# Convolution tables loaded earlier, the first two row tiles of an output projection written in two parts, and cache copies moved beside the residual's loads

## The chip, the cores and the metric

The kernel runs on one NeuronCore of a Trainium2 chip. The metric is device time in microseconds (us). The engines are PE (TensorE, the matrix products), DVE (VectorE), ACT (ScalarE), POOL (GpSimd) and SP (SyncE, which here only issues DMAs). DMAs issued by SP go through queue q1 and those issued by POOL through queue q0, the "software" queue; in the profile both show up on the same 16 DMA engines.

## What is computed

One layer of a hybrid decoder: RMSNorm, an input projection, gated linear attention and dilated attention, an output projection with residual, RMSNorm, a ConvFFN with residual, and a final RMSNorm. 544 tokens go through it: 512 of a prompt and 8 x 4 of samples. What the change touches, cut from the reference:

```python
D_MODEL = 2048; D_FF = 5504; CONV_W = 3
# o:  the attention's heads side by side, 16 blocks of 128 columns
h  = x + o @ w_out                                  # output projection and residual
u  = rmsnorm(h) @ w_up                              # 2 x 5504 columns
c  = causal depthwise conv of u, width 3, its first rows from state_ffn_conv
y  = h + (silu(gate(c)) * up(c)) @ w_dn             # down projection and residual
# k_sample, v_sample: the caches shifted by 4 rows, with the new rows put behind
```

## The kernel before, in words

All matrices are kept transposed: 128 rows of the model's width on the partitions, the 544 tokens along a row. A product in nearly full precision is made of three products of halves: each weight tile `raw` is split by ACT into `whi` (line 190) and by DVE into `wlo` (line 191), each operand likewise into a high and a low tile, and PE multiplies high by high, high by low and low by high. `wpart` loads 8 blocks of 128x128 of a weight (512 KB, issued by SP at line 846) and splits them; `gemm` (line 225) multiplies a list of such units.

A scheduler (the tile framework, with a timeline simulation) sets the order of instructions on each engine, so the order written in the program is a proposal. A DMA queue serves what is put on it in the order of issue. Tiles are allocated from pools with a fixed number of buffers, and a write waits until the buffer's last reader is done.

Four stages matter here.

- **Output projection** (about 840 to 1060 us). A loop over 16 row tiles `ot`, line 930: `gemm` of two units with the operands `og` (16 of them, of which the last two are ready last). DVE adds the PSUM tile to the residual `h`, loaded by POOL from `xT` (lines 935, 936); POOL writes the sum to `hscr` in DRAM (line 937); at every odd `ot`, `keep_rows()` puts one copy of 3060 KB, DRAM to DRAM, on POOL's queue (line 634), a piece of `k_sample` or `v_sample`. 16 such copies are made in the whole kernel, 10 of them in earlier stages and 6 here.
- **ConvFFN, up projection** (about 1060 to 1986 us). 43 pairs of column tiles. Each product (`product`, line 965) goes through the steps p1 to p7 of a `Pair`, in a fast-multiplication scheme that makes operands by additions. After the first tiles' statistics `rstd` are ready, POOL loads the convolution's table `vcv` (line 1086) and the first states `ci` (line 1101); ACT copies the states into the tiles `F` (line 1028).
- **Down projection.** First a short `gemm` over three kept pairs (16 row tiles), then three groups of pairs, each with 16 row tiles of 12 us. The activations come back from DRAM (`ar <- adr`, SP, line 1141) into `NSLOT` slots of one pool and 24 - `NSLOT` of another. In the first group the residual is added: SP loads `hr <- hscr[ot]` (line 1202), DVE adds it.
- **End.** The final norm and the outputs.

Of the kernel before, what the change touches and what calls it, by code (L numbers as in the profile page):

```python
# [17 lines left out]
P = 128  # L18
# [24 lines left out]
GATES_FIRST = 4  # L43
POOL_SPLIT = 6
NKEPT = 3
NSLOT = 11
FW = 2 + TP + NB * (2 + TS)


# [74 lines left out]
def _build(tc, nc, es, xT, st_gla, ck, cv, conv_in, vecs, w_in, w_gu, w_out, w_up, w_dn,  # L124
# [172 lines left out]
    def gps():  # L297
        return pg.tile([P, 2, 512], F32, tag="g", name="g")
# [551 lines left out]
    def wpart(w, ks, c0):  # L850
        with tc.high_priority(offset=min(PO, tc.cur_priority - P0)):
            n = len(ks)
            raw = wraw()
            wload(raw, w, ks, c0)
            hi, lo = wsplit(raw, n)
        return [(k, hi[:, i, :], lo[:, i, :]) for i, k in enumerate(ks)]
# [38 lines left out]
    def factors(some, X, pool):  # L895
# [24 lines left out]
        for i in some:  # L920
# [3 lines left out]
            else:  # L924
                parts(i, T3, 2, b[i][:, 1:3])

    X = {}
    for ot in range(KD):
        ps = gps()
        gemm(ps, [wpart(w_out, order[:8], ot * P), wpart(w_out, order[8:], ot * P)], og)  # L930
        i, j = divmod(ot, 2)
        if j == 0:
            hp = HX.tile([P, 2, NT], F32, tag="h", name="h", bufs=KD // 2 + 1 - AHEAD)
        ht = hp[:, j]
        nc.gpsimd.dma_start(ht, xT[ot * P:(ot + 1) * P, :])
        nc.vector.tensor_add(hv(ht), hv(ht), ps[:, :, :HT])
        nc.gpsimd.dma_start(hscr[ot], ht)
        if ot == 0:
            nc.scalar.activation(acc2, ht, AF.Square)
        else:  # L940
            sq = htmp("sq")
            nc.scalar.activation(sq, ht, AF.Square)
            nc.vector.tensor_add(acc2, acc2, sq)
        X[i] = hp
        if ot % 2 == 1 and kept_rows:
            keep_rows()
        nc.scalar.activation(ht, ht, AF.Copy, scale=vec[:, V_FFN + ot:V_FFN + ot + 1])
        if j == 1 and i < AHEAD:
            factors([i], X, VA)
# [27 lines left out]
    class Pair:  # L977
# [79 lines left out]
        def conv(self):  # L1057
            out = []
            for s, F in ((0, self.Fu), (1, self.Fg)):
# [22 lines left out]
    nc.scalar.activation(rstdF[:, 2:2 + TP], rstd[:, :TP], AF.Copy)  # L1082
    nc.scalar.activation(rstdF[:, 2 + TP:].rearrange("p (b s) -> p b s", s=2 + TS)[:, :, 2:],
                         rstd[:, TP:].rearrange("p (b t) -> p b t", t=TS), AF.Copy)
    vcv = FP.tile([P, NVEC - V_CW], F32, name="vcv")
    nc.gpsimd.dma_start(vcv, vecs[:, V_CW:])

    ci_v = conv_in.rearrange("p (s f) r -> p s f r", s=2)
    co_v = conv_out.rearrange("p (s f) r -> p s f r", s=2)
    def sv(x):  # L1090
        return x[:, 2 + TP:].rearrange("p (b s) -> p b s", s=2 + TS)[:, :, :TS]

    KEPT = list(range(KF - 1 - NKEPT, KF - 1))
    kept = {}
    ci = co = None
    for f, pr in enumerate(pairs):
        if f % 4 == 0:
            n = min(4, KF - f)
            ci = FP.tile([P, 2, 4, 2 * NB], F32, tag="ci", name="ci", bufs=2)
            co = FP.tile([P, 2, 4, 2 + 2 * NB], F32, tag="co", name="co", bufs=2)  # L1100
            nc.gpsimd.dma_start(ci[:, :, :n, :], ci_v[:, :, f:f + n, :])
        pr.ci, pr.co = ci[:, :, f % 4, :], co[:, :, f % 4, :]
        if f:
            pr.p5()
# [85 lines left out]
    for gi, ks in enumerate(groups):  # L1190
        A = {}
        with tc.high_priority(offset=min(2000, tc.cur_priority - P0)):
            for k in ks:
                A[k] = A1[k] if k in A1 else fetch(k, where[k])
        if gi < len(groups) - 1:
            for ot in range(KD):
                ps = gps()
                gemm(ps, [wpart(w_dn, ks[i:i + 8], ot * P) for i in range(0, len(ks), 8)], A)
                nc.vector.tensor_add(hv(h[ot]), hv(h[ot]), ps[:, :, :HT])
                if gi == 0:  # L1200
                    x = W3.tile([P, NT], F32, tag="hr", name="hr", bufs=1)
                    nc.sync.dma_start(x, hscr[ot])
                    nc.vector.tensor_add(h[ot], h[ot], x)


# [116 lines left out]
```

## Time and profile before

| | |
|---|---|
| median of 3 runs | 2526.18 us (2524.59 to 2527.97) |
| the profiled execution's own time | 2525.1 us |
| its span | 2523.3 us, so 1.8 us lie around it |
| mean granted TensorE clock | 0.991 of full speed |
| PE busy | 2462.7 us, 98% of the span |

The span is what the views of the trace cover; sums are made against the profiled execution's 2525.1 us, which is 1.1 us under the median. The granted clock is given in shares of 2.4 GHz; at its lower level, 1.2 GHz, it reads 0.5.

### The profile page before, as it was taken

The page shows a single profiled execution, that of the slowest core. Times are in us where ns is not written, and L with a number is a line of the kernel's source. Part 1 is how long each engine was busy: PE and PEld are TensorE (multiplying, and loading weights), DVE is VectorE, ACT ScalarE, POOL GpSimd, SP SyncE. Part 2 cuts the span into 40 slices and gives each one's busy share as a digit, 9 for nine tenths or more (in the row PEclk, how much of TensorE's full clock was granted, in tenths as well). Part 3 has the DMA queues.
Part 4 walks back from the last instruction along what each step waited for, and adds up shares of the span by engine and source line. Part 5 has one row for each costly group of instructions (what it writes and reads, how often), then busy time and mean ns, then how long its engine had stood idle before and what let it go on. Part 6 is the DMA issues. An engine that isn't in the chain of part 4 may idle for free.

```text
span 2523.3 us, 47163 instructions
## 1 busy us (share of the span) xinstructions
PE 2462.7 (98%) x19479; PEld 2385.2 (95%) x19479; DVE 1619.3 (64%) x2460; ACT 1078.8 (43%) x1870; POOL 435.3 (17%) x581
## 2 busy tenths in 40 slices
PE   8999999999999899989999999999999999999997
PEld 8988887899999899989999999999999999999997
DVE  7777764267777843478878888888888643342243
ACT  6344464133334433355555555555555531131142
POOL 1333434210002320112212221222121000000001
PEclk9999999999999999999999999999999999999999
DMA  7777744544555498668888888889888473443232
GB/s 220 197 202 197 193 114 138 161 131 141 166 177 177 159 305 256 169 146 192 192 188 192 191 191 189 191 191 192 189 191 178 124 219 107 115 151 92 85 100 72
DMA packets 581593, 427.73 MB, mean 170 GB/s; under 512 B 18976, under 2 KB 553728, under 8 KB 580608
## 3 DMA queue, kind: packets, MB, share of 16 engines
q1 hardware_dynamic: 462144, 248.31, 34.9%
q0 software_dynamic: 115200, 171.02, 30.1%
q10 hardware_dynamic: 4032, 5.38, 0.6%
q8 instruction: 153, 2.51, 0.4%
q14 instruction: 64, 0.52, 0.1%
HBM read 397.40 MB, written 77.37 MB: 188 GB/s over the span
## 4 chain that ended last, share of the span: by engine, by line
PE 82%; DMA 8%; DVE 6%; issue 2%; POOL 1%; ACT 1%; SPq 0%; DVEq 0%; POOLq 0%; ACTq 0%
PE g L225 40%; PE b L965 20%; PE g L965 15%; DMA q<-qscr 6%; DVE pr L411 1%; PE v L507 1%; PE s L673 1%; DMA ar<-adr 1%; DVE wlo L191 1%; DVE kv L412 1%; PE s L561 1%; DMA xr<-in_xT_dram 0%; PE s L548 0%; PE s L795 0%; POOL q L408 0%
## 5 line engine op out<-in xcount | busy, mean ns | idle before, releaser
L191 DVE TENSOR_TENSOR wlo<-raw,whi 128x1024 fp32r<-128x1024 f32 (+1 forms) x341 | 408.3, 1198 | 295.6 <-ACT whi L190 288.7
L190 ACT ACTIVATE whi<-raw 128x1024 fp32r<-128x1024 f32 (+1 forms) x345 | 355.0, 1030 | 555.1 <-PE g L225 454.0
L225 PE MATMUL g<-ah,whi 128*128 128x272 f32 x2048 | 442.9, 296 | 9.8 <-ACT ah L190 4.6
L225 PE MATMUL g<-al,whi 128*128 128x272 f32 x2048 | 447.2, 297 | 0.5 <-DVE al L191 0.5
L225 PE MATMUL g<-ah,wlo 128*128 128x272 f32 x2048 | 442.4, 295 | 0.3 <-DVE wlo L191 0.3
L965 PE MATMUL b<-vh,whi 128*128 128x272 f32 x1376 | 395.1, 288 | 6.2 <-ACT V L1038 4.8
L965 PE MATMUL b<-vl,whi 128*128 128x272 f32 x1376 | 395.9, 289 | 0.8 <-DVE vl L893 0.6
L965 PE MATMUL b<-vh,wlo 128*128 128x272 f32 x1376 | 389.9, 288 | 1.3 <-DVE wlo L191 1.3
L225 PEld LDWEIGHTS g<-ah,whi 128*128 128x128 f32 x2048 | 327.9, 191 | 19.7 <-issue 10.3
L225 PEld LDWEIGHTS g<-al,whi 128*128 128x128 f32 x2048 | 329.2, 191 | 11.6 <-issue 9.3
L225 PEld LDWEIGHTS g<-ah,wlo 128*128 128x128 f32 x2048 | 328.3, 190 | 10.2 <-issue 8.5
L965 PE MATMUL g<-vl,whi 128*128 128x272 f32 x1032 | 298.8, 290 | 2.0 <-DVE vl L893 1.9
L965 PE MATMUL g<-vh,whi 128*128 128x272 f32 x1032 | 297.8, 289 | 0.4 <-ACT vh L892 0.3
L965 PE MATMUL g<-vh,wlo 128*128 128x272 f32 x1032 | 296.8, 288 | 0.0
L965 PEld LDWEIGHTS b<-vh,whi 128*128 128x128 f32 x1376 | 260.0, 189 | 6.7 <-ACT V L1038 5.1
L225 PE MATMUL g<-dh,whi 128*128 128x272 f32 x1248 | 258.0, 288 | 4.1 <-ACT whi L190 2.7
L965 PEld LDWEIGHTS b<-vl,whi 128*128 128x128 f32 x1376 | 259.5, 189 | 1.5 <-DVE vl L893 1.5
L965 PEld LDWEIGHTS b<-vh,wlo 128*128 128x128 f32 x1376 | 257.4, 189 | 1.5 <-DVE wlo L191 1.5
L225 PE MATMUL g<-dh,wlo 128*128 128x272 f32 x1248 | 258.2, 288 | 0.0
L225 PE MATMUL g<-dl,whi 128*128 128x272 f32 x1248 | 258.1, 288 | 0.0
L190 ACT ACTIVATE whi<-rs 128x1024 fp32r<-128x1024 f32 x129 | 136.8, 1061 | 266.8 <-PE g L965 201.1
L225 PEld LDWEIGHTS g<-dh,whi 128*128 128x128 f32 x1248 | 195.7, 188 | 5.4 <-ACT whi L190 3.4
(341 smaller groups left out, 4101.5 us busy)
## 6 DMA issues: line engine op xcount, KB each, us to landing
raw<-in_w_up_dram SPq DMA_DIRECT2D x129, 512.0 KB, 4.1
raw<-in_w_in_dram SPq DMA_DIRECT2D x96, 512.0 KB, 4.8
raw<-in_w_dn_dram SPq DMA_DIRECT2D x64, 512.0 KB, 4.0
out_k_s_dram<-in_ck_dram POOLq DMA_DIRECT2D x8, 3060.0 KB, 12.7
out_v_s_dram<-in_cv_dram POOLq DMA_DIRECT2D x8, 3060.0 KB, 14.5
ra<-in_w_up_dram SPq DMA_DIRECT2D x43, 512.0 KB, 7.9
rs<-in_w_up_dram SPq DMA_DIRECT2D x43, 512.0 KB, 3.8
rs<-in_w_up_dram POOLq DMA_DIRECT2D x43, 512.0 KB, 9.8
```

Of the source, the lines that this page charges most:

```text
L190: nc.scalar.activation(hi, src, AF.Copy)
L191: eng.tensor_sub(lo, src, hi.bitcast(F32))
L225: nc.tensor.matmul(ps[:, s, :HT], a, b[:, s * HT:(s + 1) * HT], start=(i == 0 and n == 0), stop=(i == len(todo) - 1 and n == 2))
L411: nc.vector.tensor_mul(pr, kt[:, 4:5, :].broadcast_to([P, TS, QC]), q5[:, 1:5, :])
L412: nc.vector.tensor_mul(kt[:, 0:4, :], kt[:, 0:4, :], q5[:, 0:1, :].broadcast_to([P, 4, QC]))
L507: nc.tensor.matmul(psv[32 * m:32 * m + 32, :QC], lhs, rhs, start=(kt == 0), stop=(kt == 5), tile_position=(0, 32 * m))
L561: nc.tensor.matmul(psc[r, :P], vt[:, j * P + 64 * e:j * P + 64 * e + 64], t[:, j * P:(j + 1) * P], start=(j == 0), stop=(j == qi))
L673: nc.tensor.matmul(ps[:, c * P:(c + 1) * P], KS[:, c * P:(c + 1) * P], Q[:, :, c * 64:(c + 1) * 64], start=True, stop=True)
L965: nc.tensor.matmul(b[:, :HT], a_[:, i, :], x_[i][:, v, :], start=(first and i == 0 and n == 0), stop=(i == 7 and n == 2), skip_group_check ...
```

## The change

Five edits. (1) `vcv` and the first `ci` are allocated from another pool and loaded by POOL before the output projection's first `h` load; (2) the first two row tiles of the output projection are written as two passes: units up to the last two operands for both tiles, then the last two for both; (3) the six last copies leave the output projection and are issued at odd `ot` of the first group of the down projection; (4) the loads `hr` go from SP's queue to POOL's and get two buffers in place of one; (5) `NSLOT` is 10 in place of 11.

```diff
-NSLOT = 11
+NSLOT = 10
...
+    vcv = wu.tile([P, NVEC - V_CW], F32, name="vcv")
+    nc.gpsimd.dma_start(vcv, vecs[:, V_CW:])
...
+    def states(f):
+
+        n = min(4, KF - f)
+        ci = wu.tile([P, 2, 4, 2 * NB], F32, tag="ci", name="ci", bufs=2)
+        co = wu.tile([P, 2, 4, 2 + 2 * NB], F32, tag="co", name="co", bufs=2)
+        nc.gpsimd.dma_start(ci[:, :, :n, :], ci_v[:, :, f:f + n, :])
+        return ci, co
+
+    state = states(0)
+
+    def two_tiles(w, order, X, n):
+
+        out = []
+        for ot in range(2):
+            units = [u for ks in (order[:8], order[8:]) for u in wpart(w, ks, ot * P)]
+            out.append((gps(), units))
+        for part in range(2):
+            for ps, units in out:
+                m = len(units) - n
+                for i, (k, hi, lo) in list(enumerate(units))[m * part:(m, None)[part]]:
+                    xh, xl = X[k]
...
     X = {}
+    starts = two_tiles(w_out, order, og, 2)
     for ot in range(KD):
-        ps = gps()
-        gemm(ps, [wpart(w_out, order[:8], ot * P), wpart(w_out, order[8:], ot * P)], og)
+        if ot < 2:
+            ps = starts[ot]
+        else:
+            ps = gps()
+            gemm(ps, [wpart(w_out, order[:8], ot * P), wpart(w_out, order[8:], ot * P)], og)
...
-        if ot % 2 == 1 and kept_rows:
-            keep_rows()
...
-    vcv = FP.tile([P, NVEC - V_CW], F32, name="vcv")
-    nc.gpsimd.dma_start(vcv, vecs[:, V_CW:])
...
                 if gi == 0:
-                    x = W3.tile([P, NT], F32, tag="hr", name="hr", bufs=1)
-                    nc.sync.dma_start(x, hscr[ot])
+                    x = ctile("hr")
+                    if ot % 2 == 1 and kept_rows:
+                        keep_rows()
+                    nc.gpsimd.dma_start(x, hscr[ot])
                     nc.vector.tensor_add(h[ot], h[ot], x)
```

What this makes of the instructions' order is shown at three places. Line numbers of the changed kernel are about 30 higher than those of before.

The first place is the first two row tiles of the output projection. On PE, the changed kernel's rows for their last two operands (`ah_9199` and `ah_9203`, with their low halves `al_`) read:

```order
L955 MATMUL g<-ah_9199,whi 128x272 x4
L955 MATMUL g<-al_9200,whi 128x272 x2
L955 MATMUL g<-ah_9199,wlo 128x272 x2
L955 MATMUL g<-ah_9203,whi 128x272 x2
L955 MATMUL g<-al_9200,whi 128x272 x2
L955 MATMUL g<-ah_9199,wlo 128x272 x2
```

Before, these rows stand at the same numbers in the same order, with L225 for L955; so do the rows ahead of them back to the start of both tiles: the scheduler had already put the two tiles into each other. On DVE, at the evacuation of these tiles, before:

```order
L191 TENSOR_TENSOR al_9204<-oa,ah_9203 128x544
L191 TENSOR_TENSOR wlo<-raw,whi 128x1024
L936 TENSOR_TENSOR h<-h,g 128x544
L191 TENSOR_TENSOR wlo<-raw,whi 128x1024
L936 TENSOR_TENSOR h<-h,g 128x544
L943 TENSOR_TENSOR acc_9278<-acc_9278,sq 128x544
```

And changed:

```order
L191 TENSOR_TENSOR al_9204<-oa,ah_9203 128x544
L191 TENSOR_TENSOR wlo<-raw,whi 128x1024 x2
L972 TENSOR_TENSOR h<-h,g 128x544 x2
L979 TENSOR_TENSOR acc_9278<-acc_9278,sq 128x544
L191 TENSOR_TENSOR wlo<-raw,whi 128x1024
```

A second weight split now stands ahead of the first evacuation.

The second place is ACT at the first pair's end, where the states enter `F` and the next weights are split. Before:

```order
L1017 ACTIVATE U_11440<-b0_11320 128x272
L1082 ACTIVATE rstdF_11402<-rstd_77 128x512
L1083 ACTIVATE rstdF_11402<-rstd_77 128x8x4
L1028 ACTIVATE F_11472<-ci_11408 128x8x2
L1028 ACTIVATE F_11473<-ci_11408 128x8x2
L190 ACTIVATE whi_11582<-raw_11580 128x1024
L1038 ACTIVATE V_11511<-b0_11320 128x272
```

And changed:

```order
L1051 ACTIVATE U_11434<-b0_11319 128x272
L1062 ACTIVATE F_11466<-ci_9281 128x8x2
L1062 ACTIVATE F_11467<-ci_9281 128x8x2
L1116 ACTIVATE rstdF_11401<-rstd_77 128x512
L1117 ACTIVATE rstdF_11401<-rstd_77 128x8x4
L190 ACTIVATE whi_11576<-raw_11574 128x1024
L1072 ACTIVATE V_11505<-b0_11319 128x272
```

The copies from `ci` moved ahead of the two `rstdF` copies, and their load is now issued some 200 us earlier in the program.

The third place is the start of the down projection's first group. SP before, around its first residual load:

```order
L846 DMA raw_22656<-in_w_dn_dram 128x8x128
L846 DMA raw_22769<-in_w_dn_dram 128x8x128
L1141 DMA ar<-adr_9247 128x544
L1202 DMA hr<-hscr_9219 128x544
L1141 DMA ar<-adr_9248 128x544
```

In the changed kernel SP has the same rows without the `hr` row, and POOL, whose list before had nothing behind its last `adr` store but the final products, goes on like this:

```order
L1147 DMA adr_9277<-a 128x544
L1230 DMA hr<-hscr_9219 128x544
L634 DMA out_k_s_dram<-in_ck_dram 48x16320
L1230 DMA hr<-hscr_9220 128x544
L1230 DMA hr<-hscr_9221 128x544
L634 DMA out_v_s_dram<-in_cv_dram 48x16320
L1230 DMA hr<-hscr_9222 128x544
L1230 DMA hr<-hscr_9223 128x544
L634 DMA out_k_s_dram<-in_ck_dram 48x16320
```

The first `hr` load waits for PE's last product of the kept pairs; the first copy and the second `hr` load wait for nothing else; the third waits for DVE's addition of the first. So the first copy goes out right behind the first `hr` load, when the kept pairs end, and that is also when SP issues `raw_22656`.

## Rows read from the trace of the kernel before

**Rows 1.** Windows: length; busy of PE, PEld, DVE, ACT, POOL; clock, DMA share, GB/s.

```profile
900.00:1050.00 150.00, 150.00 (x1197) 150.00 (x1196) 63.02 (x86) 52.07 (x71) 14.20 (x24) 1.00 0.83 255
...
1090.00:1100.00 10.00, 5.03 (x24) 4.49 (x23) 4.28 (x6) 3.21 (x8) 2.02 (x2) 0.70 0.82 163
1100.00:1950.00 850.00, 850.00 (x6795) 850.00 (x6794) 678.97 (x929) 439.82 (x769) 169.12 (x218) 1.00 0.88 189
...
2020.00:2030.00 10.00, 9.14 (x72) 8.73 (x70) 3.40 (x4) 3.57 (x7) 0.00 (x0) 1.00 1.04 295
2030.00:2040.00 10.00, 8.69 (x55) 8.47 (x56) 4.77 (x5) 4.16 (x5) 0.00 (x0) 0.83 0.87 257
```

**Rows 2.** Timeline of PE, 1087 to 1101: start, duration, [idle before <- releaser].

```profile
1090.47 0.29 PE L965 MATMUL b<-vh,wlo 128*128 128x272 f32 x1
1095.60 0.60 PE L965 MATMUL b<-vh,whi 128*128 128x272 f32 x1 [4.85 <-ACT V L1038]
...
1097.16 0.43 PE L965 MATMUL b<-vh,wlo 128*128 128x272 f32 x1
1097.39 0.43 PE L965 MATMUL b<-vh,whi 128*128 128x272 f32 x1
```

**Rows 3.** Timeline of ACT, 1084 to 1097.

```profile
1088.48 0.64 ACT L1082 ACTIVATE rstdF<-rstd 128x512 f32<-128x512 f32 x1 [3.73 <-DVE rstdF L1081]
...
1094.00 0.32 ACT L1028 ACTIVATE F<-ci 128x16 f32<-128x16 f32 x2 [4.77 <-DMA ci<-in_conv_in_dram]
1094.23 1.04 ACT L190 ACTIVATE whi<-raw 128x1024 fp32r<-128x1024 f32 x1
1095.17 0.38 ACT L1038 ACTIVATE V<-b 128x272 f32<-128x272 f32 x1
```

**Rows 4.** Timeline of POOL, 1076 to 1099; an issuing row's duration is that of the issue.

```profile
1088.35 0.59 POOL L1086 DMA_DIRECT2D vcv<-in_vecs_dram  x1 [2.01 <-DVE rstd L171]
1088.92 0.73 POOL L1101 DMA_DIRECT2D ci<-in_conv_in_dram  x1
```

**Rows 5.** Timeline of POOL, 874 to 900.

```profile
883.48 4.31 POOL L935 DMA_DIRECT2D h<-in_xT_dram  x8 [17.29 <-issue]
```

**Rows 6.** Timeline of PE, 880 to 897.

```profile
881.56 1.27 PE L225 MATMUL g<-ah,whi 128*128 128x272 f32 x4 [4.55 <-ACT ah L190]
889.82 0.79 PE L225 MATMUL g<-ah,whi 128*128 128x272 f32 x2 [3.14 <-DVE h L936]
```

**Rows 7.** Timeline of DVE, 874 to 900.

```profile
888.95 0.72 DVE L936 TENSOR_TENSOR h<-h,g 128x544 f32<-128x544 f32 x1 [0.66 <-DMA h<-in_xT_dram]
889.59 1.22 DVE L191 TENSOR_TENSOR wlo<-raw,whi 128x1024 fp32r<-128x1024 f32 x1
```

**Rows 8.** Timeline of SP, 2012 to 2050.

```profile
2023.21 1.46 SPq L846 DMA_DIRECT2D raw<-in_w_dn_dram  x2
```

**Rows 9.** DMA issue at 2023.2: KB, us to landing.

```profile
raw<-in_w_dn_dram SPq DMA_DIRECT2D x1, 512.0 KB, 6.7
```

**Rows 10.** Timeline of ACT, 2028 to 2033.

```profile
2030.02 2.00 ACT L190 ACTIVATE whi<-raw 128x1024 fp32r<-128x1024 f32 x2 [1.09 <-DMA raw<-in_w_dn_dram]
```

**Rows 11.** Timeline of PE, 2028 to 2032.

```profile
2031.13 0.52 PE L225 MATMUL g<-dh,whi 128*128 128x272 f32 x2 [1.99 <-ACT whi L190]
```

**Rows 12.** DMA, 919.5 to 931, a copy in flight: packets, MB, share of engines.

```profile
q0 software_dynamic: 136, 3.36, 87.7%
q1 hardware_dynamic: 487, 0.25, 9.1%
```

**Rows 13.** DMA, 894 to 906, loads and a copy on q0 mixed.

```profile
q0 software_dynamic: 1402, 3.35, 95.6%
q1 hardware_dynamic: 1935, 0.97, 34.8%
```

**Rows 14.** DMA issues around 919.0: a load half a microsecond behind a copy, KB, us to landing.

```profile
out_v_s_dram<-in_cv_dram POOLq DMA_DIRECT2D x1, 3060.0 KB, 12.5
raw<-in_w_out_dram SPq DMA_DIRECT2D x1, 512.0 KB, 14.4
```

More of the change, by code (lines that the diff above doesn't have):

```diff
@@ L925, in factors @@
                 parts(i, T3, 2, b[i][:, 1:3])
+    vcv = wu.tile([P, NVEC - V_CW], F32, name="vcv")
+    nc.gpsimd.dma_start(vcv, vecs[:, V_CW:])
+    ci_v = conv_in.rearrange("p (s f) r -> p s f r", s=2)
+    co_v = conv_out.rearrange("p (s f) r -> p s f r", s=2)
+    def states(f):
[15 more added lines that the diff above has]
+                    xh, xl = X[k]
+                    for j, (a, b) in enumerate(((hi, xh), (hi, xl), (lo, xh))):
+                        for s in range(2):
+                            nc.tensor.matmul(ps[:, s, :HT], a, b[:, s * HT:(s + 1) * HT], start=(i == 0 and j == 0),
+                                             stop=(i == len(units) - 1 and j == 2), skip_group_check=True)
+        return [ps for ps, units in out]
     X = {}
+    starts = two_tiles(w_out, order, og, 2)
     for ot in range(KD):
-        ps = gps()
-        gemm(ps, [wpart(w_out, order[:8], ot * P), wpart(w_out, order[8:], ot * P)], og)
+        if ot < 2:
[3 more added lines that the diff above has]
+            gemm(ps, [wpart(w_out, order[:8], ot * P), wpart(w_out, order[8:], ot * P)], og)
         i, j = divmod(ot, 2)
@@ L1084, in _build @@
                          rstd[:, TP:].rearrange("p (b t) -> p b t", t=TS), AF.Copy)
-    vcv = FP.tile([P, NVEC - V_CW], F32, name="vcv")
-    nc.gpsimd.dma_start(vcv, vecs[:, V_CW:])
-    ci_v = conv_in.rearrange("p (s f) r -> p s f r", s=2)
-    co_v = conv_out.rearrange("p (s f) r -> p s f r", s=2)
     def sv(x):
@@ L1094, in _build @@
     kept = {}
-    ci = co = None
     for f, pr in enumerate(pairs):
         if f % 4 == 0:
[L1098 to L1101, printed above, removed]
+            ci, co = states(f) if f else state
         pr.ci, pr.co = ci[:, :, f % 4, :], co[:, :, f % 4, :]
```

## The prediction, made before the changed kernel ran

> **What bounds the kernel now.** The page says that PE is busy for 98% of the span; about 60 us are idle, so what this change can give lies in a few waits of PE and in the clock behind them. I therefore read the busy windows by stage first, to see where PE waits at all, then the timelines around each wait, and last the DMA queues. The windows [rows 1] show two long stretches with nothing to win: the output projection from 900 to 1050 and the up projection from 1100 to 1950 have PE busy to the last hundredth at full clock. 150 us hold 1197 matmuls there, so a matmul costs 0.125 us at full clock. In 1090 to 1100 PE is busy for 5.03 us only, at a clock of 0.70; in 2020 to 2040 it idles too, and the DMA engines are saturated (share 1.04, 295 GB/s) as nowhere else in these rows. These two places, with the start of the output projection, are the ones where the edits land.
>
> **Edit 1, the early table and states: a gain of 6.2 us.** PE stops after the matmul at 1090.47 and goes on at 1095.60, having waited 4.85 us for ACT's `V` [rows 2]. On ACT [rows 3] `V` stands behind the split `whi`, and that behind the copies `F<-ci`, which waited 4.77 us for the states' DMA. POOL issued it at 1088.92, just after the table, because `vcv` had waited for `rstd` [rows 4]. In the changed kernel the states are loaded 200 us earlier, so `F<-ci` waits for nothing but `rstd`, which is there before 1088.48. What is late next: the split `whi` of 1.04 us needs a buffer that PE's running product reads until shortly before its end, and `V` (0.38 us) needs that end itself, 1090.47 + 0.29 = 1090.8. If `whi` runs from 1090.1 to 1091.2, `V` ends at 1091.55 and PE goes on at about 1091.6. Its wait shrinks from 4.85 to 0.8: 4.05 us. Then the clock: the matmuls behind the long wait come every 0.23 us (1097.16, 1097.39 [rows 2]), which is the level of 1.2 GHz. The 24 matmuls of that window would take 3.0 us at 0.125 instead of 5.03, which is 2.0 lost; with an estimated 0.2 for the first ones behind 1100 it is 2.2 us, which I count as gained, since a wait of 0.8 us is short. Sum 6.2. Ends: 3.5, if half of the wait's remainder stays with another operand and the clock falls all the same (4.85 - 1.35); 7.05, if nothing is left at all. The up projection behind it is PE-bound [rows 1], so the gain is kept.
>
> The same edit puts the table and two loads of states ahead of the first `h` load on POOL's queue. POOL stood idle ahead of those loads for 17 us and began them at 883.48 [rows 5]. The three new issues take 0.59 + 0.73 + 0.73 = 2.05 us; how much of that fits into the idle time depends on when their buffers come free, so the `h` load is late by 0 to 2.05 us. What this costs is taken with the next edit, where the load is waited for.
>
> **Edit 2, two tiles in two passes: 0, with a loss of 0.7 beside it.** PE waits 4.55 us up to 881.56 for the last operands and 3.14 us up to 889.82 for the first evacuation [rows 6]. The passes would fill the first wait if PE took up other work there. But the instructions on PE stand in the same order as before, the two tiles being already interleaved: both waits have what they had ahead of them. On DVE, the second `wlo` (1.22 us) now stands ahead of the first evacuation, which had ended at 889.67 after waiting 0.66 us for its residual's load [rows 7], the one that POOL issues from 883.48 on. If that `wlo` starts where DVE had been waiting, at about 888.29, it ends at 889.5 and the evacuation starts 0.55 us later than before; the later load adds a little if it is late by more than 0.5. I take +0.7; ends 0 and +2.05.
>
> **Edit 3 at its old place: 0.** The copies delayed loads there, but PE waited for nothing from 900 to 1050 [rows 1]; a quicker load gives nothing.
>
> **Edits 3 and 4 at their new place: a loss of 9 us.** The kept pairs' products end at about 2023.2. SP then issues two weight loads, at 2023.21 [rows 8]; the first takes 6.7 us [rows 9], ACT starts to split it at 2030.02 after 1.09 us of waiting [rows 10], and PE stands still for 1.99 us until 2031.13 for that split [rows 11]. So here a DMA ends last, and every microsecond that this load comes later is one more for PE, which has done by then what it could do without it. The first `hr` load on POOL is released by the same event, takes 0.55 us to issue, and the first copy follows, at about 2023.8 to 2024.3. It brings 3.13 MB to engines that are full.
>
> How much the copy holds up the load is the disputed price. With a copy alone on q0 [rows 12], 11.5 us moved 3.36 MB for q0 and 0.25 MB for q1: 292 and 22 GB/s. The copy's 3.13 MB take 10.7 us, in which q1 gets 0.24 MB in place of the 3.15 MB of 295 GB/s, so that it is thrown back by 9.9 us. With small-row loads mixed into q0 [rows 13] q1 got 0.97 MB in 12 us, 81 GB/s, which throws it back by 10.7 - 2.9 = 7.8 us. The `hr` load's 272 KB, earlier than before, add up to 0.9. A load of 512 KB issued half a microsecond behind a copy landed after 14.4 us [rows 14], 7.7 later than the 6.7 of ours. These say 7.7 to 10.8; I take 9, because our load has something like 2 us of head start before the copy's data move. Ends: 0, if it lands before; 13.4, if the copy's whole 12.5 us of issue to landing and the 0.9 lie ahead.
>
> The Trainium skill's page "DMA: Bandwidth & Descriptors" says in its section "Queues, rings and completion order" that each DMA engine takes turns between the queue rows at the granularity of packets, so that big packets take more of it. Our rows agree in kind: per packet in the trace q0 moved 25 KB and q1 0.5 KB, although the turns were not equal in number (136 to 487). Read as equal shares of the bytes the rule would make this loss about 4.5, not 9.
>
> The clock behind this wait is already 0.83 in 2030 to 2040 [rows 1], so a longer wait adds little there. Later copies come every 24 us behind an addition of DVE, the rhythm which the output projection bore at 150 of 150 us [rows 1], and the third and later `hr` loads have 24 us for themselves: 0. What covers them is the weights' buffers, filled ahead; if that cover is gone, each of the five costs what the first does.
>
> **Edit 5: 0.** The number of loads is the same and their order on SP keeps its rows; PE's order takes 60 matmuls of the second row tile ahead of the last operands of the first, so a late activation has 7.5 us of cover.
>
> **Sum.** -6.2 + 0.7 + 0 + 9 + 0 = +3.5 us. On the profiled execution's 2525.1 that is 2528.6; its median stands 1.1 us higher, so the forecast for the median is 2529.7, rounded to 2529.5. About 5 us (0.2%) is what a measurement of this kernel can tell from no change, so the likeliest outcome is "the same, a little slower".
>
> **Rivals**, all as medians (2526.2 plus the sum).
>
> - *Even shares.* The load and the copy share the engines evenly. The load has about 4.6 us left when the copy's data start, and needs twice that: +4.5, sum -1.0, 2525.2. For it: nothing in the rows except that q1 had 81 GB/s once. Chance 0.15.
> - *The load is out before.* The copy's data start too late to touch it (over 5 us behind its issue), or another weight's buffer bridges it: sum -5.5, 2520.7, faster. For it: the load is issued first, by half a microsecond or more. Against: the 14.4 us of the load at 919.0, and the wait of 1.99 us, which says that nothing bridges it now. Chance 0.16.
> - *The copy's whole way lies ahead* (the other side). +13.4 in place of 9, sum +7.9, 2534.1. It decides "slower" from a landing more than 10.6 us later, that is from 2040.5 on in the old time. For it: q1 nearly stands still in rows 12, and what the load has behind it in the queue (the second weight unit, the next activation) comes later still. Chance 0.25.
> - *The two passes do what they are written for* and fill the 4.55 us: the forecast's sum less 4.55, so -1.0, 2525.2. Against: PE's unchanged order. Chance 0.04.
>
> **How the numbers follow.** The forecast has 0.40. Its own range, from a loss of 7.7 to one of 10.8 and a gain of 5.5 to 6.5, is 2528 to 2532.2. The range of 8 in 10 takes in the two outer rivals' centres: 2520 to 2535. Faster by over 0.2% comes from the second rival and the luckier part of the two near zero: 0.18. Slower by over 0.2% comes from the third rival and the upper edge of the forecast: 0.32. The same: 0.50.
>
> **What would show it.** Right: no idle of PE over 1.5 us around 1090 and the clock at 1.0 behind it; PE's two waits around 880 and 890 as before within 1 us; the load issued at the kept pairs' end landing after 14 to 17 us, and a PE wait of 10 to 12 us at about 2031, for `whi`; no waits of PE at the later copies. Wrong: a PE wait under 5 us at 2031, a second one near 2060, or a wait at 1090 that merely changes its releaser.

## The result, and the profile after

The changed kernel is slower: 2543.0 us median of 4 runs (2540.3 to 2544.0), against 2525.4 us (2524.2 to 2528.0) for the kernel before; ratio 1.0067, 95% interval 1.0049 to 1.0084. The forecast was 2529.5 with a range up to 2535.0, so it was wrong: the sign of the sum was right, its size was not. The profiled execution took 2542.5 us, its span 2540.7 us, 17.4 us longer than the span before.

What PE waited for in the changed kernel, from the view of its waits (total us, times, longest):

```profile
PE g L225 <- ACT whi L190: 15.1, 4, 11.3
...
PE g L225 <- DVE h L972: 4.9, 1, 4.9
PE g L955 <- ACT ah L190: 4.6, 1, 4.6
...
PE g L225 <- ACT h L1182: 2.1, 3, 1.1
...
PE b L999 <- ACT V L1072: 0.8, 1, 0.8
```

The first row is the new stall at the down projection, the last what is left of the 4.85 us of [rows 2]. The row on `h` of L972 and the one on `ah` answer to [rows 6]. Now the places of these waits on PE's timeline in the changed kernel:

```profile
829.58 1.13 PE L673 MATMUL s<-QB,KB 128*128 128x128 f32 x8 [2.18 <-DVE QB L669]
...
884.13 1.27 PE L955 MATMUL g<-ah,whi 128*128 128x272 f32 x4 [4.55 <-ACT ah L190]
893.69 0.49 PE L225 MATMUL g<-ah,whi 128*128 128x272 f32 x2 [4.90 <-DVE h L972]
1070.07 0.39 PE L999 MATMUL b<-vh,whi 128*128 128x272 f32 x1 [1.36 <-ACT V L1035]
1094.21 0.39 PE L999 MATMUL b<-vh,whi 128*128 128x272 f32 x1 [0.81 <-ACT V L1072]
2042.98 0.82 PE L225 MATMUL g<-dh,whi 128*128 128x272 f32 x2 [11.27 <-ACT whi L190]
2096.30 0.52 PE L225 MATMUL g<-dh,whi 128*128 128x272 f32 x2 [0.81 <-ACT whi L190]
2527.82 0.72 PE L1242 MATMUL v<-sq,onesD 128*128 128x272 f32 x2 [0.53 <-ACT sq L1256]
```

and three rows of the same view of the kernel before that were not shown yet:

```profile
827.04 1.47 PE L673 MATMUL s<-QB,KB 128*128 128x128 f32 x8 [2.18 <-DVE QB L669]
...
1067.42 0.39 PE L965 MATMUL b<-vh,whi 128*128 128x272 f32 x1 [1.38 <-ACT V L1001]
...
2509.92 0.73 PE L1214 MATMUL v<-sq,onesD 128*128 128x272 f32 x2 [0.53 <-ACT sq L1228]
```

A stall list alone does not explain 17.4 us. For that one needs marks at which both kernels do the same thing. One good mark is ACT's copy `U`, once in each pair of the up projection; here are the copies of the second and of the last pair, in the changed kernel:

```profile
1108.39 0.38 ACT L1051 ACTIVATE U<-b 128x272 f32<-128x272 f32 x1
...
1974.63 0.38 ACT L1051 ACTIVATE U<-b 128x272 f32<-128x272 f32 x1
```

and in the kernel before:

```profile
1111.56 0.38 ACT L1017 ACTIVATE U<-b 128x272 f32<-128x272 f32 x1
...
1973.16 0.38 ACT L1017 ACTIVATE U<-b 128x272 f32<-128x272 f32 x1
```

The 41 pairs between them take 861.60 us before and 866.24 us after. PE has no wait in that stretch in either kernel. With the rows above, the span divides like this:

| stretch | before, us | after, us | difference | forecast |
|---|---|---|---|---|
| start to the wait at 827 | 827.04 | 829.58 | +2.5 | 0 |
| to `U` of the second pair | 284.52 | 278.81 | -5.7 | -5.5 |
| 41 pairs, to `U` of the last | 861.60 | 866.24 | +4.6 | 0 |
| to the final norm on PE | 536.76 | 553.19 | +16.4 | +9 |
| to the end | 13.38 | 12.88 | -0.5 | 0 |
| span | 2523.3 | 2540.7 | +17.4 | +3.5 |

So the second line came out as forecast; the third has a loss where nothing was forecast; the fourth is nearly twice as large as its term; and the first, ahead of every edit, is chance, as the profiles of the experiments show: the same mark stood anywhere from 822.7 to 830.0 in them.

The windows of the changed kernel, by the columns of [rows 1]:

```profile
900.00:1050.00 150.00, 150.00 (x1197) 150.00 (x1196) 62.67 (x85) 53.05 (x71) 11.35 (x19) 1.00 0.45 129
1090.00:1100.00 10.00, 8.77 (x68) 8.33 (x67) 5.43 (x9) 4.08 (x10) 1.68 (x3) 1.00 0.92 173
1100.00:1950.00 850.00, 850.00 (x6761) 850.00 (x6760) 679.21 (x928) 439.21 (x769) 168.94 (x218) 1.00 0.88 189
```

From 900 to 1050 the copies are gone (DMA share 0.45 instead of 0.83), and PE did the same 1197 matmuls. At 1090 the clock stays at 1.00. From 1100 to 1950 PE is as busy as before at the same granted clock, and yet does 6761 matmuls where it did 6795: each one takes 0.5% longer. Busy shares cannot show that; counts can.

At the start of the down projection, POOL's timeline in the changed kernel, with the first and the third copy:

```profile
2025.98 0.54 POOL L1230 DMA_DIRECT2D hr<-hscr  x1 [29.68 <-PE g L225]
2026.52 0.53 POOL L634 DMA_DIRECT2D out_k_s_dram<-in_ck_dram  x1
...
2079.73 0.52 POOL L634 DMA_DIRECT2D out_k_s_dram<-in_ck_dram  x1
```

and the DMA view from 2025.5 to 2036.5 (packets, MB, share; then KB and us to landing):

```profile
q0 software_dynamic: 126, 3.28, 78.5%
q1 hardware_dynamic: 1821, 1.13, 35.8%
...
out_k_s_dram<-in_ck_dram POOLq DMA_DIRECT2D x1, 3060.0 KB, 13.8
raw<-in_w_dn_dram SPq DMA_DIRECT2D x2, 512.0 KB, 16.7
```

Of the weight loads, the first is issued at 2025.71, 0.8 us ahead of the copy; the two together have a median of 16.7 us, and the first alone, by the DMA view from 2025.6 to 2026, has

```profile
raw<-in_w_dn_dram SPq DMA_DIRECT2D x1, 512.0 KB, 16.1
```

in place of the 6.7 of [rows 9]: 9.4 us more.

### The profile page after: what moved, and what is told of

Read it like the earlier page. It is cut to its first block, busy times and chain, and to the rows that moved or that the text cites. A ratio compares the mean times of both kernels' runs of the same rounds, so it can differ in the third digit from the quotient of the medians.

```text
span 2540.7 us, 47169 instructions
## 1 busy us (share of the span) xinstructions
PE 2466.6 (97%) x19479; PEld 2389.5 (94%) x19479; DVE 1619.9 (64%) x2460; ACT 1079.5 (42%) x1870; POOL 443.5 (17%) x597
## 4 chain that ended last, share of the span: by engine, by line
PE 81%; DMA 9%; DVE 6%; issue 2%; ACT 1%; POOL 1%; SPq 0%; DVEq 0%; ACTq 0%; POOLq 0%
PE g L225 38%; PE b L999 20%; PE g L999 15%; DMA q<-qscr 6%; DMA ar<-adr 2%; DVE pr L411 1%; PE v L507 1%; PE s L673 1%; DVE wlo L191 1%; DMA raw<-in_w_dn_dram 1%; PE g L955 1%; PE s L561 1%; DVE kv L412 1%; PE s L548 0%; DMA xr<-in_xT_dram 0%
## 5 line engine op out<-in xcount | busy, mean ns | idle before, releaser
L191 DVE TENSOR_TENSOR wlo<-raw,whi 128x1024 fp32r<-128x1024 f32 (+1 forms) x341 | 407.8, 1197 | 288.5 <-ACT whi L190 281.4
L225 PE MATMUL g<-ah,whi 128*128 128x272 f32 x1984 | 427.4, 294 | 7.7 <-DVE h L972 4.9
L225 PE MATMUL g<-al,whi 128*128 128x272 f32 x1984 | 431.5, 296 | 0.0
L225 PE MATMUL g<-ah,wlo 128*128 128x272 f32 x1984 | 426.7, 294 | 0.0
L225 PEld LDWEIGHTS g<-ah,whi 128*128 128x128 f32 x1984 | 315.8, 189 | 17.0 <-issue 11.6
L225 PEld LDWEIGHTS g<-al,whi 128*128 128x128 f32 x1984 | 317.2, 190 | 10.4 <-issue 9.1
L225 PEld LDWEIGHTS g<-ah,wlo 128*128 128x128 f32 x1984 | 316.6, 190 | 9.3 <-issue 8.1
L225 PE MATMUL g<-dh,whi 128*128 128x272 f32 x1248 | 260.0, 291 | 15.8 <-ACT whi L190 12.6
L225 PE MATMUL g<-dl,whi 128*128 128x272 f32 x1248 | 259.2, 289 | 0.0
L225 PE MATMUL g<-dh,wlo 128*128 128x272 f32 x1248 | 258.2, 288 | 0.5 <-DVE wlo L191 0.5
L225 PEld LDWEIGHTS g<-dh,whi 128*128 128x128 f32 x1248 | 195.3, 189 | 17.8 <-ACT whi L190 13.3
```

Source lines behind the costliest of these rows:

```text
L191: eng.tensor_sub(lo, src, hi.bitcast(F32))
L225: nc.tensor.matmul(ps[:, s, :HT], a, b[:, s * HT:(s + 1) * HT], start=(i == 0 and n == 0), stop=(i == len(todo) - 1 and n == 2))
```

## The experiments

The changes below are edits of the kernel before or of the changed one; medians stand beside runs of the kernel before on the same chip, whose medians were 2522.9 to 2524.0. Five kernels only add an unused tile. "A pair" is the time between the second and the last `U`, divided by 41; "16 row tiles" is the time between DVE's additions that close the 16th and the 32nd row tile of the down projection, a stretch in which PE waits in none of the kernels and the granted clock is 1.00.

| kernel | median, us | ratio to before, 95% | a pair, us | 16 row tiles, us |
|---|---|---|---|---|
| changed, 32 bytes more | 2533.6 | 1.0044 (1.0030 to 1.0058) | 21.014 | 192.74 |
| before, 32 bytes more | 2527.3 | 1.0015 (1.0006 to 1.0025) | 21.135 | 192.00 |
| early loads alone | 2518.4 | 0.9984 (0.9975 to 0.9994) | 21.015 | 192.74 |
| copies moved alone | 2585.6 | 1.0249 (1.0233 to 1.0264) | 21.015 | 192.04 |
| two passes alone | 2522.9 | 0.9996 (0.9987 to 1.0006) | 21.014 | 192.04 |
| first copy later | 2521.9 | 0.9993 (0.9984 to 1.0003) | 21.015 | 192.74 |
| copies back | 2521.8 | 0.9995 (0.9985 to 1.0004) | 21.014 | 192.74 |
| first copy in short rows | 2529.8 | 1.0024 (1.0014 to 1.0033) | 21.014 | 192.74 |
| before, 64 bytes more | 2523.7 | 1.0003 (0.9993 to 1.0012) | 21.001 | 192.10 |
| bytes behind the operands | 2523.9 | 1.0004 (0.9995 to 1.0013) | 21.015 | 192.05 |
| residual on POOL alone | 2525.7 | 1.0011 (1.0002 to 1.0021) | 21.014 | 192.05 |
| first copy in four long parts | 2532.1 | 1.0038 (1.0025 to 1.0051) | 21.015 | 192.74 |
| second half moved | 2522.6 | 0.9992 (0.9984 to 1.0001) | 20.981 | 192.04 |
| left side moved | 2525.0 | 1.0003 (0.9994 to 1.0012) | 20.981 | 192.58 |
| early loads, left side moved | 2519.0 | 0.9977 (0.9967 to 0.9987) | 20.981 | 192.59 |

Before and changed have 21.015 and 21.128 us a pair, and 192.04 and 193.18 us for the 16 row tiles.

**Where do the 4.6 us in the up projection come from?** The table and the states went into a pool that is allocated ahead of others on the same side of the memory. They take 3552 bytes a partition, 32 more than a multiple of 64, and everything allocated behind them moved by that. So the first half of the up projection's operands (`vh0` to `vh3`, `vl0` to `vl3`), which began at addresses of 32 modulo 64, now begin at multiples of 64. Theory A says that this sets the pace; its rivals are chance and the shift as such. Two kernels, one from each side; first the changed kernel with 32 bytes more:

```diff
-    vcv = wu.tile([P, NVEC - V_CW], F32, name="vcv")
-    nc.gpsimd.dma_start(vcv, vecs[:, V_CW:])
+    vcv = wu.tile([P, NVEC - V_CW + 8], F32, name="vcv")
+    nc.gpsimd.dma_start(vcv[:, :NVEC - V_CW], vecs[:, V_CW:])
```

> The changed kernel with 32 bytes more in the table's tile, so that the operand tiles allocated behind it begin at an address of 32 modulo 64 again, as before the change, instead of 0. Theory A (the start address of the operands, modulo 64 bytes, sets the matmul's pace): the 41 pairs of the up projection go back from 21.13 to 21.01 us each, the matmuls of the down projection from 125.6 to 125.0 ns, and the kernel is 6 to 8 us faster than the changed one, near 2535.5. Theory B (the pace belongs to the run or the chip, not to the program): no difference from the changed kernel by the program, 2541 to 2544, and the pace as its neighbours in the same batch have it. Theory C (it is the shift by 3552 bytes as such, through which engine meets which in the same part of the memory): still 21.13 us, about 2542, since the shift is now 3584.

Then the kernel before with 32 bytes more:

```diff
+    pad = wu.tile([P, 8], F32, name="pad")
+    nc.gpsimd.memset(pad, 0.0)
     X = {}
     for ot in range(KD):
```

> The kernel before with an unused tile of 32 bytes ahead of the same operands; nothing else differs. Theory A: slower by 6 to 8 us, about 2532.5, with 21.13 us for a pair in place of 21.01. Theory B: 2525, 21.01 us or whatever its neighbours show. Theory C: 2525, since a shift of 32 bytes brings no engine into another part of the memory.

The pace of the up projection switched both ways. The kernel before with 32 bytes more:

```profile
1110.89 0.38 ACT L1019 ACTIVATE U<-b 128x272 f32<-128x272 f32 x1
...
1977.41 0.38 ACT L1019 ACTIVATE U<-b 128x272 f32<-128x272 f32 x1
```

866.52 us for the 41 pairs, 4.9 more than without the bytes, from an unused tile; and the changed kernel with 32 bytes more is back at 21.014. Chance and the shift as such are out. In the whole time the effect is at the edge of the noise: by the ratios the bytes give the changed kernel 0.23%, 5.8 us, just under the 6 to 8 us that theory A asked for, with intervals that overlap; they cost the kernel before 4.4 us in the medians, less than it asked for. And theory A had also claimed the down projection, and there it is wrong. Its 16 row tiles before, between these two additions of DVE,

```profile
2219.74 0.72 DVE L1199 TENSOR_TENSOR h<-h,g 128x544 f32<-128x544 f32 x1 [2.17 <-PE g L225]
...
2411.78 0.72 DVE L1199 TENSOR_TENSOR h<-h,g 128x544 f32<-128x544 f32 x1 [3.94 <-PE g L225]
```

and in the changed kernel

```profile
2236.20 0.72 DVE L1225 TENSOR_TENSOR h<-h,g 128x544 f32<-128x544 f32 x1 [2.69 <-PE g L225]
...
2429.38 0.72 DVE L1225 TENSOR_TENSOR h<-h,g 128x544 f32<-128x544 f32 x1 [3.97 <-PE g L225]
```

take 192.04 and 193.18 us; with the bytes they take 192.00 and 192.74. All six kernels with 10 slots and the 32 bytes alone (copies and passes as they may be) show 192.74: most of that loss comes with the 10 slots, or with the table's new place that always went with them here, not with the 32 bytes.

Two controls narrow it down, 64 bytes in the same place, and 32 bytes allocated behind the operands:

```diff
+    pad = wu.tile([P, 16], F32, name="pad")
...
+    pad = RE.tile([P, 8], F32, name="pad")
```

> The kernel before with an unused tile of 64 bytes ahead of the up projection's operands, which then start at 32 modulo 64 as before, but at 32 modulo 128 in place of 96. If the start modulo 64 bytes sets the pace: 21.01 us for a pair and the time of before within 2 us. If it is the start modulo 128 (the fast kernels all stood at 96, the slow ones at 0 and 64): over 21.05 us for a pair, and slower by 2 us or more.

> The kernel before with 32 unused bytes behind the operands and the weights' buffers of the up projection: the operands stay where they were, and the tiles that DVE, ACT and POOL work on there (F, c, ci, the table, the residual's h, the kept pairs' operands) move by 32 bytes. If the pace hangs on PE's own operands: 21.01 us for a pair and the time of before within 2 us. If it hangs on the other engines' tiles, which moved along in the slow kernels: 21.13 us and 4 to 6 us slower.

Neither is slower: 21.001 and 21.015 us. So it is not the tiles of the other engines behind the operands, and 64 bytes more do no harm. What stayed in its place in the second control are the first half of PE's operands and, behind them, two weight buffers (pool `RE`), which PE does not read but which had moved in both slow kernels too. The traces settle this one: `RE` holds the weights of every other pair only, those between lie in a pool that moved in neither, and yet each pair loses the same: summed over products of 24 matmuls, the loss repeats pair by pair to within 2 ns a product. So it is the start of PE's own operands. How the loss is spread over the seven products of a pair differs: 0 to 36 ns a product in the changed kernel, 10 to 27 in the kernel before with 32 bytes, for the same sum of some 0.12 us. The last question was whether 32 modulo 64 is the better start for any operand. The second half of the operands (`vh4` to `vh7`) starts at multiples of 64 in the kernel before:

```diff
     vb_p, VB = opened(name="vb", bufs=1)
+    pad = VB.tile([P, 8], F32, name="pad")
+    nc.gpsimd.memset(pad, 0.0)
```

> The kernel before with 32 unused bytes ahead of the second half of the up projection's operands (blocks 4 to 7), which then start at 32 modulo 64 like the first half; nothing else moves. If 32 modulo 64 is the faster start for any operand: 20.90 us for a pair in place of 21.01, and 4 to 5 us faster than before. If the two halves must differ, or the first half is a case of its own: 21.01 or more, and no gain.

It is not: the pair took 20.981 us, 0.033 less, where a rule for every operand would have given another 0.11. And with the whole left side of the memory moved by 32 bytes:

```diff
+    left = cons.tile([P, 8], F32, name="left")
+    nc.gpsimd.memset(left, 0.0)
     acts_p, acts = opened(name="acts", bufs=1)
```

> The kernel before with 32 unused bytes at the base of the memory's left side, so that the operands of the input and output projections, the second half of those of the up projection, and the first pool of the down projection's operands all start at 32 modulo 64. If the rule holds for any operand: 20.90 us for a pair; under 191.5 us in place of 192.04 for 16 row tiles of the down projection, half of whose operands move; and 5 to 9 us faster than before in all. If it holds for the up projection alone: 4 to 5 us faster. If not even there: no gain.

the up projection has the same 20.981, the 16 row tiles of the down projection take 192.58 instead of 192.04, and nothing is gained in all. Theory A in its general form falls. That 32 bytes more at the start of the first half cost 0.12 us a pair, and 64 nothing, is shown; why, and what the rule is for other operands, stays open.

**The early loads alone**, which need the 10 slots, with the 32 bytes:

> Only the early loads of the table and the states (with the 32 bytes, and 10 slots, which they need room for); copies, residual loads and row tiles as before. By the changed kernel's trace the wait at 1090 falls from 4.85 to 0.8 us and the clock stays up: faster than before by 5 to 6.5 us, 2519 to 2520.5. If the early loads have a price of their own at the first row tiles (the wait for the first evacuation was 4.9 in place of 3.1 us), 1.8 less: 2521 to 2522. If theory A is wrong and the shift itself costs, 2526.

```profile
1090.19 0.39 PE L980 MATMUL b<-vh,whi 128*128 128x272 f32 x1 [0.81 <-ACT V L1053]
```

The wait is 0.81 us, as in the changed kernel, and this kernel is faster than before by 0.16%, 4.6 us in the medians: just under the 5 to 6.5 that were expected, with 0.7 us lost in the 16 row tiles. With the left side moved as well:

> The kernel with the early loads alone, with the same 32 bytes at the base of the left side. By the sum of what its two parts give: 5 us from the early loads and what the bytes give in the run beside it; 9 to 13 us faster than before if the rule holds, 5 if it doesn't. In the down projection with 10 slots: 192.74 us for 16 row tiles if the pace there hangs on something else, less if it hangs on the same.

0.9977 is the best ratio measured, but its interval overlaps that of the early loads alone, and the 9 to 13 us of the rule did not come. Its 16 row tiles take 192.59 us, as with 11 slots and the left side moved (192.58): there 10 slots cost nothing, so the 0.7 us from above is no price of the slots as such; it hangs on where the tiles of the down projection lie.

**The copies alone**, on the kernel before:

```diff
-        if ot % 2 == 1 and kept_rows:
-            keep_rows()
...
+                    if ot % 2 == 1 and kept_rows:
+                        keep_rows()
                     nc.sync.dma_start(x, hscr[ot])
```

> Only the six copies moved to the down projection's first group; the residual's loads stay on SP's queue, nothing else changes, no address moves. If the first copy holds up the weight load behind which PE waits: a wait of 9 to 12 us in place of 2 near 2031, and the kernel slower than before by 9 to 14 us, 2534 to 2539. If the residual load ahead of the copy on the same queue was what kept the copy back, the copy now starts earlier and the wait is longer still. If the copies are harmless by themselves and only the residual's loads on the same queue hurt: 2525 to 2527.

```profile
2050.95 0.82 PE L225 MATMUL g<-dh,whi 128*128 128x272 f32 x2 [50.01 <-ACT whi L190]
```

One wait of 50 us, with shorter ones behind it (the longest 4.24 us); the kernel is 62.6 us slower than before. Without the residual's loads among them, nothing on POOL's queue held the copies back: all six were issued between 1989.5 and 1992.6, while the kept pairs still ran, and they cost 8.3 us each on average (50.0 / 6) in this wait alone. That is the price of a copy that lies ahead of needed loads, six times over; the expectation had thought of an earlier copy, not of six. It also shows what the residual's loads on POOL do in the changed kernel: they meter the copies.

**The first copy later**, on the changed kernel with 32 bytes more:

```diff
-                    if ot % 2 == 1 and kept_rows:
+                    if ot % 2 == 1 and ot > 4 and kept_rows:
                         keep_rows()
```

> The changed kernel with the 32 bytes, in which the six copies stand at the row tiles 5, 7, ... 15 of the down projection's first group in place of 1, 3, ... 11. If the loss is that of a first copy which runs into the loads that the group's start waits for, and the later ones hide: the wait of 11.4 us goes, at most 2 us are left in its place, and the kernel is 9 to 11 us faster than with the 32 bytes alone, about 2523 on the chip of the last batch and 2 to 4 us slower than with the early loads alone. If any copy beside these weight loads costs: the wait moves to the place of the new first copy, and the gain is under 4 us.

```profile
2022.37 0.52 PE L225 MATMUL g<-dh,whi 128*128 128x272 f32 x2 [3.38 <-ACT whi L190]
```

The wait of 11.44 us is 3.38, no other of over 0.2 us follows before the final norm, and the kernel is 0.5% (11.7 us) faster than with the bytes alone. The first copy now leaves here:

```profile
2057.02 0.53 POOL L634 DMA_DIRECT2D out_k_s_dram<-in_ck_dram  x1
```

44 us behind the group's first residual load (2013.25). So six copies beside the down projection cost next to nothing, and the one that starts with it costs nearly all.

**What are the other 3.4 us?** The same kernel with the copies put back into the output projection:

> The changed kernel with the 32 bytes and the copies back in the output projection; the residual's loads stay on POOL's queue with two buffers, and the two passes stay. If the queue of the residual's loads and the passes do not matter: as the early loads alone, 4 to 6 us faster than before. If the residual's loads on the software queue disturb the weight loads at the group's start: a wait of over 3 us near 2030 and the time of before.

has a wait of 3.18 us there without any copy near it, and the same time (2521.8). The residual's loads alone on POOL, on the kernel before:

```diff
-                    x = W3.tile([P, NT], F32, tag="hr", name="hr", bufs=1)
-                    nc.sync.dma_start(x, hscr[ot])
+                    x = ctile("hr")
+                    nc.gpsimd.dma_start(x, hscr[ot])
```

> The kernel before with the residual's loads alone moved to POOL's queue and given two buffers; copies, table and row tiles as before. If the two loads, which go out as soon as the kept pairs end, take the engines from the weight loads: the wait at 2031 grows from 2 to 3 or 4 us, and the kernel is 1 to 3 us slower. If they do nothing: a wait of 1.3 to 2 us there and the time of before within 1 us.

```profile
2034.33 0.77 PE L225 MATMUL g<-dh,whi 128*128 128x272 f32 x2 [2.85 <-ACT whi L190]
```

2.85 us in place of 1.99, and 0.11% (2.6 us) slower. In the kernels whose edits leave the queues of this stage alone the wait is 1.2 to 2.3 us; in the three with the residual on POOL and no copy near, it is 2.85 to 3.4. So the edit that was costed at 0.9 us inside the copy's price has a price of about 1 to 3 us by itself: two loads of 272 KB leave as soon as the kept pairs end, 0.3 us behind the weights for which PE waits.

**How does a copy hold a load up?** The forecast rested on the length of the pieces. On the changed kernel with 32 bytes more, the first copy alone in four DMAs, once by quarters of the columns (pieces of 768 bytes), once by quarters of the rows (long pieces):

```diff
-        tc.keep_in_program_order(nc.gpsimd.dma_start(dst[b, 0:PAST - TS, :], src[b, TS:PAST, :]))
+        w = src.shape[2] // n
+        for c in range(n):
+            c = slice(c * w, c * w + w)
+            tc.keep_in_program_order(nc.gpsimd.dma_start(dst[b, 0:PAST - TS, c], src[b, TS:PAST, c]))
...
+        w = (PAST - TS) // n
+        for r in range(0, PAST - TS, w):
+            tc.keep_in_program_order(nc.gpsimd.dma_start(dst[b, r:r + w, :], src[b, TS + r:TS + r + w, :]))
```

> The changed kernel with the 32 bytes, in which the first of the six copies is made of four DMAs that each move a quarter of the columns, so that its contiguous pieces are 768 bytes long in place of 65 KB; the bytes are the same. If the copy starves the other queue because its packets are some fifty times as long: now that they are of the same order as those of the weight loads, the weight load issued beside it lands after 9 to 13 us in place of 16 to 17, the wait of 11.4 us falls to 4 to 8, and the kernel is 4 to 7 us faster than with the 32 bytes alone. If the bytes alone count, or the order in which the DMAs were issued: the wait stays at 10 to 12 us. If short pieces only make the copy slower on all engines: the wait grows.

> The control to the copy in short pieces: the first copy again as four DMAs that take POOL as long to issue, but each moves a quarter of the rows, in long contiguous pieces. If the length of the pieces is what starves the weight loads: a wait of 10 us or more is back near 2030, and the time is that of the changed kernel with the 32 bytes, 9 to 11 us slower than before. If it was the later issue or the splitting into four that helped: waits of 4 to 7 us in sum, as with the short pieces.

The DMA queues in 11 us that begin 1.2 us (short pieces, shown first) and 1.7 us (long pieces) after the first of the four issues:

```profile
q0 software_dynamic: 596, 2.45, 60.4%
q1 hardware_dynamic: 2190, 1.32, 41.6%
```

and with long pieces:

```profile
q0 software_dynamic: 211, 3.46, 83.6%
q1 hardware_dynamic: 1025, 0.59, 18.6%
```

The two weight loads issued beside the copy, KB and us to landing, again short pieces first:

```profile
raw<-in_w_dn_dram SPq DMA_DIRECT2D x2, 512.0 KB, 11.8
```

```profile
raw<-in_w_dn_dram SPq DMA_DIRECT2D x2, 512.0 KB, 18.0
```

And PE's waits, in the same order:

```profile
2026.40 0.52 PE L225 MATMUL g<-dh,whi 128*128 128x272 f32 x2 [2.34 <-ACT whi L190]
2036.66 0.82 PE L225 MATMUL g<-dh,whi 128*128 128x272 f32 x2 [4.01 <-ACT dh L190]
```

```profile
2033.22 0.82 PE L225 MATMUL g<-dh,whi 128*128 128x272 f32 x2 [12.67 <-ACT whi L190]
```

With long pieces the stall is 12.7 us; with short ones, and the same bytes, 2.3 and then 4.0 for an activation, and q1 moved more than twice as much meanwhile (1.26 MB in the window that begins 1.7 us after the issue as well). The split into four by itself does nothing. Two reservations: the short pieces took POOL 3.1 us to issue and the long ones 2.0, so their last part starts a little later; and in the whole time the short pieces gain 2.3 us on the long ones, with intervals that just overlap, so it is the waits that show it.

**The two passes alone**, on the kernel before:

> The kernel before with the first two row tiles written in two passes, and nothing else. If the passes do nothing because PE's order was already so: PE's wait of 4.55 us near 882 stays, the wait for the first evacuation is 3 to 4 us, and the time is that of before within 2 us. If the passes do what they are written for: the wait of 4.55 us falls below 1 us, and the kernel is 3 to 4.5 us faster.

PE's waits for `ah` and for the first evacuation were 4.55 and 3.01 us, and the time that of before. The passes do nothing.

## Why the prediction was wrong

**Edit 1 was right.** The stretch from 827 to the second pair changed by -5.7 us for a forecast of -6.2 + 0.7. The remaining wait is 0.81 us (0.8 was forecast), the clock stayed at 1.00. The +0.7 for the first evacuation hid two errors: PE's wait there grew by 1.8 us, not 0.7, because `h` came later, behind the table and the states. This DVE row of the changed kernel shows the wait for the load:

```profile
892.82 1.35 DVE L972 TENSOR_TENSOR h<-h,g 128x544 f32<-128x544 f32 x2 [1.30 <-DMA h<-in_xT_dram]
```

The delay came with the early loads, not with the passes: from the end of the wait for `ah` to PE's restart behind the evacuation it is 8.26 us before, 8.35 with the two passes alone, 9.41 with the early loads alone and 9.56 in the changed kernel. And almost all was given back before 1070, where the clock was lower for a shorter time: 0.67 and 0.70 in the windows 880 to 890 and 890 to 900 before, 0.83 in both after. From the wait at 881.6 to the one at 1067.4 PE takes 185.86 us before and 185.94 after (884.13 to 1070.07).

**Edit 2 was right** (0, shown by the two passes alone), and so was **edit 3 at its old place**: the same 1197 matmuls in the same 150 us.

**Edits 3 and 4 at their new place: the mechanism and the stall were right, the term was too small.** The wait grew by 9.28 us (11.27 - 1.99) for a forecast of 9, by the weight load which was named. The rival of even shares is out for this copy: a load with 9.4 us more to landing is near to what [rows 12] say, and only the copy in short pieces came near to sharing. What the term left out are the things that follow. Between the last `U` and the final norm PE waited 16.7 us in all after and 4.6 before (all its rows with a wait in that stretch added up), 12.1 more: the stall, 0.7 for another wait ahead of it, and 2.3 in four small ones from 2062 to 2098 that the kernel before has not. The prediction had 0 for the later copies; two of the four, 1.3 us, come 16.6 us behind the third copy's issue (2079.73 on POOL's timeline above), and with the first copy later there are none. That a longer wait adds little to the clock's loss behind it was right: the clock is 0.66 from 2043 to 2050 after, and 38 matmuls were done in these 7 us, which at full clock are 4.8: 2.2 lost there, where before 8.87 us behind the wait held 55 matmuls (6.9) and a further wait of 0.18, so that 1.8 were lost. That is 0.4 more, little, as forecast. The rest of the 16.4 us, about 4, is pace for the most part: 193.18 against 192.04 us for 16 row tiles are 0.6%, which over the 530 us of this stretch would be an estimated 3 us.

**Edit 5 at 0 was wrong**, together with the table's new place, by some 0.4% of the down projection: the kernels with 10 slots need 192.74 us for these 16 row tiles, or 193.18 without the 32 bytes. For the whole down projection (its first and second group and a shorter last one) 0.4% is an estimated one to two microseconds. The prediction had looked at the loads' number and order, and not at where the operands lie; that this is what counts, and not the number of slots, is what the two kernels with the left side moved say (192.58 with 11 slots, 192.59 with 10).

**What failed** is therefore the step that has no sentence of its own: the sum took the durations of before for all that the edits don't touch. "The up projection behind it is PE-bound, so the gain is kept" was the place for it. PE-bound was right; but the time of a matmul is not a constant, and moving the table into another pool changed it by 0.5% for 41 pairs: +4.6 us, shown by 32 bytes from both sides. In the down projection the same step failed by the estimated 3 us above; that the pace is lower there is measured, its cause is open. The second step that failed, a smaller one, is the 0 for what follows the stall: 2.3 us of further waits there. Of the 13.9 us between forecast and span, 4.6 are the pace of the up projection, 7.4 the fourth line of the table beyond its 9 (further waits, clock and pace), and 2.5 the stretch ahead of all edits, which is chance; the table's second and last line give 0.7 back.

On a rule that was weighed: what the Trainium skill says, that the DMA engines take turns between queues packet by packet ("DMA: Bandwidth & Descriptors", section "Queues, rings and completion order") agrees with the runs in kind: long pieces left q1 with 0.59 MB in 11 us, short ones with 1.32 MB. Read as equal shares of the bytes it would have given a loss of 4.5 us; the trace has a stall 9.28 us longer and contradicts that reading.

## What to carry to other kernels

A large copy that nobody waits for should not start where a stage's first loads start: here the same six copies cost 11 us or next to nothing, depending on whether the first one leaves with the stage or some 44 us into it; and if it must start there, short pieces hurt less than long ones did (PE waits of 2.3 and 4.0 us against 12.7). Before taking a stretch as untouched, compare the addresses of PE's operands in both programs: a tile put into another pool moves all that is allocated behind it. And compare counts of matmuls per window, not only busy shares and the clock, since both can read the same while the pace differs.

## What the runs showed of the hardware

- The pace of matmuls can depend on where their operands lie: 21.00 to 21.015 us for a pair of the up projection with the first half of its operands from byte 129376, 129312 or 125792 of a partition on (32 modulo 64), 21.13 from 129344 or 125824 on (0 modulo 64), and 20.98 with the other half moved by 32 too. The granted clock reads 1.00 in all of them. In the down projection the differences have another pattern: 192.0 to 192.1 us for 16 row tiles with 11 slots, 192.7 to 193.2 with 10, and 192.6 with either number when the left side is moved.
- A DRAM-to-DRAM copy in long pieces leaves the other queue little: 0.59 MB in 11 us, against 1.32 MB beside the same bytes in pieces of 768.
